# A hybrid decoder layer: the sample states are multiplied as they were loaded, in float32 and by column groups, and the new value's share is added at the end

## The chip, the cores and the metric

The kernel runs on one core of a Trainium2 chip. The metric is the device time of one execution in microseconds (us), lower is better. A measurement is the median of several runs. One execution was taken with the hardware profiler; its span is the time from the first to the last instruction of the program, and its own time is a little longer.

## The reference

One layer of a decoder is computed for a prompt of 512 tokens and for eight samples of one token each, which share all weights: 520 columns of activations in all, d_model 1024. The layer has one input projection, a dilated sliding-window attention (A), a gated linear attention (B), a merge by gates, an output projection, and a feed-forward block with squared relu; then a final RMSNorm. The change lies mainly in B for the samples:

```python
def gla_recurrent(q, k, v, g, s0):
    def step(state, inp):
        qt, kt, vt, gt = inp
        state = jnp.exp(gt)[..., None] * state + kt[..., None] * vt[:, :, None, :]
        return state, jnp.einsum('bhd,bhdv->bhv', qt, state)
...
def rmsnorm(x, g):
    xf = x.astype(jnp.float32)
    y = xf * lax.rsqrt(jnp.mean(xf * xf, axis=-1, keepdims=True) + EPS)
    return (y * g.astype(jnp.float32)).astype(x.dtype)
```

There are eight samples and four heads; a state is 128 x 256 float32 (128 KB), so that 32 states, 4 MB, are read, updated and written back. With a = exp(g), the output is o = q (diag(a) S + k v), which is also (q * a) S + (q . k) v.

## The kernel before

**Layout.** Activations lie with features on the 128 partitions, as tiles of 8 x 520 columns; the 520 columns are two halves of 260 (256 prompt tokens and four samples each). Weights come as panels of 128 output columns: `load_panel` fetches 512 KB on SP's queue, `split_panel` (L78) makes a high part on ACT (L90) and the rest on DVE (L91), and `panel_mms` (L106) multiplies in three passes of fp32r matmuls (L124), 48 matmuls of 260 columns a panel. TensorE goes through 140 panels in this way, and the rest of the work is woven between them.

**Fillers.** Work beside the panels stands in Python generators. `fill` (L130) takes steps of the generators in turn, `rate` steps after each panel; a step ends at `yield`. In the stage of B, `heads()` steps through `gla` (the prompt's chunked form, four heads after one another) and `samples()` through `gla_s` (L662) and `gla_s_out`, at four steps a panel; a generator that isn't ready yields True and costs no step.

**Order.** All instructions are handed to a planner, which sets the order on each engine by a simulated timeline, with the order of the program as priority. On the chip, each engine takes its instructions in the planned order and waits at each for its semaphores. A DMA stands in the queue of the engine that issues it: loads on SP's, the outputs of states and the cache copies on POOL's.

**gla_s, by head.** The preparing step makes the decay `a` (128 x 8) from the gate, copies k and q of the samples to `kq`, transposes v to rows (L679) and writes them to a DRAM tile `dV`. The next step makes `qs`, where q of a sample stands as a high and a low column of a 16-column weight, the others zero (L685 to L687). Then, for each pair of samples, the states are loaded to `st` (`sst`, two buffers, L692), the value rows are broadcast to `vb` (L693), ACT multiplies vb by k (L696), DVE makes the new state in `st` (L697), ACT and POOL split it into hi and lo in the buffer `gx` (L701, L702), four matmuls (L706) add to `po`, and POOL issues the output of `st` (L708). At the head's end `po` (16 x 256) is copied (L711), transposed (L714), and the high and low halves are added to `oS` (L715).

**The start.** `start` (L192) loads x in eight tiles and the first panels, and splits x times the norm's weight into `uh` (ACT, L211) and `ul` (DVE, L212). `stats` (L218) squares x on ACT (L223, L224), adds pairs on DVE (L225), and sums over partitions with a matmul by ones (L227), in four sets. `late_consts` (L232) loads seven small constants on POOL's queue. `rsqrt` (L174) makes v = scale * ss + eps on DVE (L179), Ln and Exp on ACT, and a Newton step on DVE.

**The end.** For each half, after the last panels (L968), the squares are summed (L979, L980), `rsqrt` gives `rs`, and `dd` is multiplied by it, six tiles on DVE and two on POOL (L985), with an output for each two tiles (L987).

Of the kernel before, what the change touches and what calls it, by code (L numbers as in the profile page):

```python
# [9 lines left out]
F32 = mybir.dt.float32  # L10
# [34 lines left out]
class Build:  # L45
# [116 lines left out]
    def pace(self, n=1):  # L162

        for _ in range(n):
            if self.copies:
                o, i = self.copies.pop(0)
                c = self.nc.gpsimd.dma_start(o, i)
                if self.last is not None:
                    self.tc.add_manual_dep(
                        c.ins, self.last.ins.name,  # L170
                        mybir.DependencyInfo(mybir.DependencyClass.Sync, mybir.DependencyReason.DATA),
                        reason="pace")

    def rsqrt(self, pool, out, ss, n, scale, np_=P):  # L174
# [3 lines left out]
        a = pool.tile([P, n], F32, tag=f"ra{n}", name="ra")  # L178
        nc.vector.tensor_scalar(v[:np_], ss, scale, EPS, op0=ALU.mult, op1=ALU.add)  # L179
        nc.scalar.activation(a[:np_], ss, AF.Ln, scale=scale, bias=self.eps[:np_])  # L180
# [11 lines left out]
    def start(self):  # L192
# [17 lines left out]
        for k in range(KT):  # L210
            nc.scalar.activation(self.uh[:, k], xr[:, k], AF.Copy, scale=self.g("n1", k))  # L211
# [6 lines left out]
    def stats(self, ap, xr):  # L218
        nc = self.nc
        pr = self.ps.tile([P, 2, 512], F32, tag="rps", name="rps")  # L220
        for k in range(0, KT, 2):
            a, b = (ap.tile([P, NT], F32, tag="sq", name="sq", bufs=5) for _ in range(2))
            nc.scalar.activation(a, xr[:, k], AF.Square)  # L223
            nc.scalar.activation(b, xr[:, k + 1], AF.Square)  # L224
            nc.vector.tensor_tensor(a, a, b, op=ALU.add)  # L225
            for j in range(2):
                nc.tensor.matmul(pr[:, j, :HC], self.ones, a[:, j * HC:(j + 1) * HC], start=(k == 0), stop=(k == KT - 2))  # L227
# [4 lines left out]
    def late_consts(self):  # L232
        nc, cp, I = self.nc, self.cp, self.I
        for n in ("ident", "maskN", "maskC", "qmask", "hsel", "dmask", "lmask"):
            a = I[n]
            t = cp.tile(list(a.shape), U8 if n == "lmask" else F32, tag=n, name=n)
            nc.gpsimd.dma_start(t, a)
# [424 lines left out]
    def gla_s(self, gp):  # L662
        nc, I, O = self.nc, self.I, self.O
        oS = gp.tile([P, 4, 2, NB], F32, tag="oS", name="oS", bufs=1)
        for h in range(4):
# [10 lines left out]
            vs = gp.tile([P, 2, 256], F32, tag="svb", name="vs", bufs=2)[:NB, 0]  # L676
# [4 lines left out]
            nc.sync.dma_start(dV, vs)  # L681
            yield

            qs = self.gx[:, :16 * NB]
            nc.scalar.activation(qs, self.ones, AF.Copy, scale=0.0)  # L685
            nc.scalar.activation(qs[:, 0::17], kq[:, 1], AF.Copy)
            nc.vector.tensor_tensor(qs[:, 8::17], kq[:, 1], qs[:, 0::17].bitcast(F32), op=ALU.subtract)  # L687
            po = self.bank("gso")
            for bp in range(4):
                st = gp.tile([P, 2, 256], F32, tag="sst", name="sst", bufs=2)  # L690
                vb = gp.tile([P, 2, 256], F32, tag="svb", name="svb", bufs=2)
                nc.sync.dma_start(st, I["state"][2 * bp:2 * bp + 2, h].rearrange("b d v -> d b v"))  # L692
                nc.sync.dma_start(vb, dV[2 * bp:2 * bp + 2].unsqueeze(0).to_broadcast([P, 2, 256]))  # L693
                for i in range(2):
                    b = 2 * bp + i
                    nc.scalar.activation(vb[:, i], vb[:, i], AF.Copy, scale=kq[:, 0, b:b + 1])  # L696
                    nc.vector.scalar_tensor_tensor(st[:, i], st[:, i], a[:, b:b + 1], vb[:, i],  # L697
                                                   op0=ALU.mult, op1=ALU.add)
                x = P + 1024 * (bp % 2)
                hi, lo = (self.gx[:, y:y + 512].rearrange("p (i v) -> p i v", i=2) for y in (x, x + 512))  # L700
                nc.scalar.activation(hi, st, AF.Copy)  # L701
                nc.gpsimd.tensor_tensor(lo, st, hi.bitcast(F32), op=ALU.subtract)  # L702
                for i in range(2):
                    b = 2 * bp + i
                    for n, w in enumerate((hi, lo)):
                        nc.tensor.matmul(po[:16, :256], qs[:, 16 * b:16 * b + 16], w[:, i],  # L706
                                         start=(b == 0 and n == 0), stop=(b == NB - 1 and n == 1))
                nc.gpsimd.dma_start(O["sgla"][2 * bp:2 * bp + 2, h].rearrange("b d v -> d b v"), st)  # L708
                yield
            o16 = gp.tile([P, 256], F32, tag="state", name="o16", bufs=2)[:16]  # L710
            nc.scalar.activation(o16, po[:16, :256], AF.Copy)  # L711
            pt = self.bank("gsp")
            for x in range(2):
                nc.tensor.transpose(pt[:, 16 * x:16 * x + 16], o16[:, x * P:(x + 1) * P], self.c["ident"][:16, :16])  # L714
            nc.vector.tensor_reduce(oS[:, h], pt[:, :32].rearrange("p (x n b) -> p x b n", x=2, n=2), axis=AX, op=ALU.add)  # L715
            yield
        sq = gp.tile([P, 4, 2, NB], F32, tag="sqS", name="sqS", bufs=1)
        nc.vector.tensor_tensor(sq, oS, oS, op=ALU.mult)
# [34 lines left out]
    def run(self):  # L753
# [74 lines left out]
        def gla_parts():  # L828
# [4 lines left out]
            self.gx = self.big("gx", F32R).rearrange("p a b -> p (a b)")  # L833
# [46 lines left out]
        with pool("late") as p:  # L880
# [75 lines left out]
            for j in range(2):  # L956
# [26 lines left out]
                for k in range(KT):  # L983
                    eng = nc.gpsimd if k >= 6 else nc.vector
                    eng.tensor_tensor(dd[:, k, cc], dd[:, k, cc], rs, op=ALU.mult)  # L985
                    if k % 2:
                        nc.sync.dma_start(O["yT"][:, k - 1:k + 1, cc], dd[:, k - 1:k + 1, cc])  # L987
# [148 lines left out]
```

## Time and profile before

| what | value |
|---|---|
| median of 3 runs | 969.25 us (967.69 to 971.42) |
| the profiled execution's own time | 968.6 us |
| its span | 966.8 us |
| busy: PE, DVE, ACT, POOL | 928.8, 556.5, 389.8, 102.3 us |
| mean granted clock of TensorE | 0.985 |
| DMA | 155.28 MB, mean 161 GB/s |

The page of the profile shows the span in 40 slices, with a digit for the busy tenths of each engine and for the granted clock in tenths of full speed, and the chain of work that ended last by engine and line. Matmuls are pipelined, so that a matmul's own duration (about 0.28 us) is longer than the time from its start to the next one's. Rows of a group end with the idle time of the engine just before its instructions, and with what ended it; a row of the timeline has start, duration, engine and line, and in brackets the idle time before it. PE is TensorE's matmul, PEld its weight load, SPq, ACTq and POOLq are the queues of the issuing engines.

### The profile page before, as it was taken

To read this page: it belongs to the slowest core of one execution; us is meant where nothing else is said; L and a number is where in the kernel's file an instruction comes from. 1 tells how busy PE (TensorE), PEld (TensorE's weight loads), DVE (VectorE), ACT (ScalarE), POOL (GpSimd) and SP (SyncE) were. 2 spreads that over 40 slices of the span, in tenths; PEclk is the share of its full clock that TensorE was granted. 3 is DMA by queue.
4 is the path that set the end of the run, shared out by engine and by line. 5 is a ranking of instruction groups with operands and counts; after the bars stand their busy time and mean duration, and the time that the engine had idled before them with its cause. 6 is when DMAs were issued, how large, how long until landed. Compare 5 with 4: busy or idle time off the path is not lost.

```text
span 966.8 us, 19936 instructions
## 1 busy us (share of the span) xinstructions
PE 928.8 (96%) x8288; PEld 909.0 (94%) x8288; DVE 556.5 (58%) x1075; ACT 389.8 (40%) x760; POOL 102.3 (11%) x148
## 2 busy tenths in 40 slices
PE   6999999999998999899899999999999999999994
PEld 6999999999898988789899999999999999999993
DVE  6657747645866946748665556443443344555654
ACT  6233243352644545556633444422432243224532
POOL 1000000001323322311000000010000000000000
PEclk9999999998999999899999999999999999999997
DMA  7455735322445344211468776778775222323311
GB/s 237 149 200 201 227 114 189 111 66 70 154 133 180 116 149 147 78 53 64 160 240 305 261 262 218 278 265 306 262 261 197 88 87 90 108 88 109 110 46 44
DMA packets 38988, 155.28 MB, mean 161 GB/s; under 512 B 5561, under 2 KB 11969, under 8 KB 36946
## 3 DMA queue, kind: packets, MB, share of 16 engines
q1 hardware_dynamic: 33778, 95.26, 28.7%
q0 software_dynamic: 4976, 58.74, 17.7%
q8 instruction: 65, 1.06, 0.5%
q14 instruction: 25, 0.20, 0.1%
q10 hardware_dynamic: 144, 0.01, 0.0%
HBM read 140.66 MB, written 54.17 MB: 202 GB/s over the span
## 4 chain that ended last, share of the span: by engine, by line
PE 83%; DMA 5%; DVE 4%; issue 3%; POOL 2%; ACT 2%; SPq 0%; DVEq 0%; POOLq 0%; ACTq 0%
PE mps L124 69%; PE mps L968 5%; PE pvp L358 1%; DMA svb<-dV 1%; DMA sst<-in_state 1%; POOL gx L702 1%; DMA raw<-in_w_in 1%; PE ptp L347 1%; DMA QTt<-ro 1%; DMA out_sgla<-sst 1%; PE spO L151 1%; PE vps L298 1%; DVE wlo L91 1%; POOL out_sgla L708 1%; PE sps L332 0%
## 5 line engine op out<-in xcount | busy, mean ns | idle before, releaser
L90 ACT ACTIVATE whi<-raw 128x512 fp32r<-128x512 f32 x264 | 165.7, 629 | 361.3 <-PE mps L124 309.7
L91 DVE TENSOR_TENSOR wlo<-raw,whi 128x512 fp32r<-128x512 f32 x264 | 184.8, 701 | 148.9 <-ACT whi L90 147.3
L124 PE MATMUL mps<-uh,whi 128*128 128x260 f32 x928 | 194.4, 289 | 7.4 <-ACT whi L90 5.5
L124 PE MATMUL mps<-ul,whi 128*128 128x260 f32 x928 | 195.8, 290 | 0.0
L124 PE MATMUL mps<-uh,wlo 128*128 128x260 f32 x928 | 193.2, 288 | 0.0
L124 PEld LDWEIGHTS mps<-uh,whi 128*128 128x128 f32 x928 | 145.8, 191 | 8.4 <-ACT whi L90 5.5
L124 PEld LDWEIGHTS mps<-ul,whi 128*128 128x128 f32 x928 | 146.5, 191 | 2.6 <-issue 1.4
L124 PEld LDWEIGHTS mps<-uh,wlo 128*128 128x128 f32 x928 | 146.2, 191 | 1.8 <-issue 1.1
L124 PE MATMUL mps<-hh,whi 128*128 128x260 f32 x512 | 103.2, 283 | 0.0
L124 PE MATMUL mps<-hh,wlo 128*128 128x260 f32 x512 | 103.2, 283 | 0.0
L124 PE MATMUL mps<-hl,whi 128*128 128x260 f32 x512 | 103.0, 283 | 0.0
L124 PEld LDWEIGHTS mps<-hh,whi 128*128 128x128 f32 x512 | 79.0, 188 | 0.1
L124 PEld LDWEIGHTS mps<-hh,wlo 128*128 128x128 f32 x512 | 78.9, 188 | 0.0
L124 PEld LDWEIGHTS mps<-hl,whi 128*128 128x128 f32 x512 | 78.7, 188 | 0.0
L124 PE MATMUL mps<-fh,wlo 128*128 128x260 f32 x384 | 77.3, 283 | 0.0
L124 PE MATMUL mps<-fl,whi 128*128 128x260 f32 x384 | 77.2, 283 | 0.0
L124 PE MATMUL mps<-fh,whi 128*128 128x260 f32 x384 | 76.8, 282 | 0.0
L124 PEld LDWEIGHTS mps<-fh,wlo 128*128 128x128 f32 x384 | 59.2, 188 | 0.0
L124 PEld LDWEIGHTS mps<-fl,whi 128*128 128x128 f32 x384 | 59.0, 188 | 0.0
L124 PEld LDWEIGHTS mps<-fh,whi 128*128 128x128 f32 x384 | 59.0, 188 | 0.0
L968 PE MATMUL mps<-fh,lw 128*128 128x260 f32 x256 | 46.6, 283 | 0.0
L968 PEld LDWEIGHTS mps<-fh,lw 128*128 128x128 f32 x256 | 39.6, 188 | 0.1
(330 smaller groups left out, 1377.6 us busy)
## 6 DMA issues: line engine op xcount, KB each, us to landing
raw<-in_w_in SPq DMA_DIRECT2D x57, 512.0 KB, 3.6
raw<-in_w_up SPq DMA_DIRECT2D x32, 512.0 KB, 4.2
raw<-in_w_down SPq DMA_DIRECT2D x32, 512.0 KB, 4.6
sst<-in_state SPq DMA_DIRECT2D x16, 256.0 KB, 2.7
svb<-dV SPq DMA_DIRECT2D x16, 256.0 KB, 3.5
out_sgla<-sst POOLq DMA_DIRECT2D x16, 256.0 KB, 3.7
raw<-in_w_pb SPq DMA_DIRECT2D x8, 512.0 KB, 4.4
raw<-in_w_o SPq DMA_DIRECT2D x8, 512.0 KB, 5.7
```

The lines of the kernel that those rows point to most:

```text
L90: nc.scalar.activation(hi, raw[:, x:x + n], AF.Copy)
L91: nc.vector.tensor_tensor(lo, raw[:, x:x + n], hi.bitcast(F32), op=ALU.subtract)
L124: self.last = nc.tensor.matmul(out[j], w, x[:, k, j * HC:(j + 1) * HC], start=(k == 0 and n == 0), stop=(k == kt - 1 and n == 2))
L151: self.nc.tensor.matmul(*args, **kw)
L298: nc.tensor.transpose(pt[:, r * P:(r + 1) * P], vt[:, r * P:(r + 1) * P], self.c["ident"])
L347: nc.tensor.transpose(pt[:, hh, x], prs[hp][:, hh, x * P:(x + 1) * P], self.c["ident"])
L358: nc.tensor.matmul(po[:, hh * 64:hh * 64 + 64], prT[:, hh, x], v, start=(x == first), stop=(x == 1))
L702: nc.gpsimd.tensor_tensor(lo, st, hi.bitcast(F32), op=ALU.subtract)
L708: nc.gpsimd.dma_start(O["sgla"][2 * bp:2 * bp + 2, h].rearrange("b d v -> d b v"), st)
L968: nc.tensor.matmul(ps, w, x[:, kk, cc], start=(kk == 0 and n == 0), stop=(kk == KT - 1 and n == 2))
```

## The change

In `gla_s`, q times the decay stands in `qz`, a weight of 32 columns a sample, of which one is not zero. It multiplies the state as it was loaded, in float32, and four samples write to the four groups of 32 output partitions of `po`, the two halves of the samples to its two halves of 256 columns. The decayed and updated state is written over `vb`, which is what goes out. States and value rows of four samples are loaded at once (512 KB each), into halves of a large buffer `sx` that takes the place of `gx`, one step of the generator ahead of their use. At a head's end, `po` is copied whole and transposed in four blocks, of which every 32nd column is kept. After the last head, q . k is summed by a matmul with ones, and multiplied by v and added to `oS`.

The other edits: Ln is put ahead of v in `rsqrt`; the odd tiles' squares of x go to POOL, and four squares are added before the sum by ones, so that there are two sets of it; the seven constant loads wait for the last split of x; at the end, DVE multiplies two tiles of `dd` at a time, and POOL none.

```diff
     def rsqrt(self, pool, out, ss, n, scale, np_=P):
...
+        nc.scalar.activation(a[:np_], ss, AF.Ln, scale=scale, bias=self.eps[:np_])
         nc.vector.tensor_scalar(v[:np_], ss, scale, EPS, op0=ALU.mult, op1=ALU.add)
-        nc.scalar.activation(a[:np_], ss, AF.Ln, scale=scale, bias=self.eps[:np_])
         nc.scalar.activation(out, a[:np_], AF.Exp, scale=-0.5)
...
         for k in range(0, KT, 2):
-            a, b = (ap.tile([P, NT], F32, tag="sq", name="sq", bufs=5) for _ in range(2))
+            a, b = (ap.tile([P, NT], F32, tag="sq", name="sq", bufs=6) for _ in range(2))
             nc.scalar.activation(a, xr[:, k], AF.Square)
-            nc.scalar.activation(b, xr[:, k + 1], AF.Square)
+            nc.gpsimd.tensor_tensor(b, xr[:, k + 1], xr[:, k + 1], op=ALU.mult)
             nc.vector.tensor_tensor(a, a, b, op=ALU.add)
+            if k % 4 == 0:
+                first = a
+                continue
+            nc.vector.tensor_tensor(a, a, first, op=ALU.add)
             for j in range(2):
-                nc.tensor.matmul(pr[:, j, :HC], self.ones, a[:, j * HC:(j + 1) * HC], start=(k == 0), stop=(k == KT - 2))
+                nc.tensor.matmul(pr[:, j, :HC], self.ones, a[:, j * HC:(j + 1) * HC], start=(k == 2), stop=(k == KT - 2))
...
-            nc.gpsimd.dma_start(t, a)
+            self.after(nc.gpsimd.dma_start(t, a), self.split_x)
...
     def gla_s(self, gp):
...
+        qz = gp.tile([P, NB, 32], F32, tag="qz", name="qz", bufs=1)
+        nc.gpsimd.memset(qz, 0.0)
+        qk = gp.tile([P, 4, NB], F32, tag="qk", name="qk", bufs=1)
...
             nc.sync.dma_start(dV, vs)
+
+            nc.vector.tensor_tensor(qz[:, :, 0], kq[:, 1], a, op=ALU.mult)
+            nc.vector.tensor_tensor(qk[:, h], kq[:, 1], kq[:, 0], op=ALU.mult)
             yield
-
-            qs = self.gx[:, :16 * NB]
-            nc.scalar.activation(qs, self.ones, AF.Copy, scale=0.0)
-            nc.scalar.activation(qs[:, 0::17], kq[:, 1], AF.Copy)
-            nc.vector.tensor_tensor(qs[:, 8::17], kq[:, 1], qs[:, 0::17].bitcast(F32), op=ALU.subtract)
             po = self.bank("gso")
-            for bp in range(4):
...
+            for bh in range(2):
+                bs = slice(4 * bh, 4 * bh + 4)
+                st, vb = (self.sx[:, x:x + 1024].rearrange("p (b v) -> p b v", b=4)
+                          for x in (1024 * bh, 2048 + 1024 * bh))
+                nc.sync.dma_start(st, I["state"][bs, h].rearrange("b d v -> d b v"))
+                nc.sync.dma_start(vb, dV[bs].unsqueeze(0).to_broadcast([P, 4, 256]))
+                yield
+
+                for i in range(4):
+                    nc.tensor.matmul(po[32 * i:32 * i + 32, 256 * bh:256 * bh + 256], qz[:, 4 * bh + i], st[:, i],
+                                     start=True, stop=True)
+                for i in range(4):
+                    b = 4 * bh + i
                     nc.scalar.activation(vb[:, i], vb[:, i], AF.Copy, scale=kq[:, 0, b:b + 1])
-                    nc.vector.scalar_tensor_tensor(st[:, i], st[:, i], a[:, b:b + 1], vb[:, i],
+                    nc.vector.scalar_tensor_tensor(vb[:, i], st[:, i], a[:, b:b + 1], vb[:, i],
                                                    op0=ALU.mult, op1=ALU.add)
-                x = P + 1024 * (bp % 2)
-                hi, lo = (self.gx[:, y:y + 512].rearrange("p (i v) -> p i v", i=2) for y in (x, x + 512))
-                nc.scalar.activation(hi, st, AF.Copy)
-                nc.gpsimd.tensor_tensor(lo, st, hi.bitcast(F32), op=ALU.subtract)
-                for i in range(2):
-                    b = 2 * bp + i
-                    for n, w in enumerate((hi, lo)):
-                        nc.tensor.matmul(po[:16, :256], qs[:, 16 * b:16 * b + 16], w[:, i],
-                                         start=(b == 0 and n == 0), stop=(b == NB - 1 and n == 1))
-                nc.gpsimd.dma_start(O["sgla"][2 * bp:2 * bp + 2, h].rearrange("b d v -> d b v"), st)
+                nc.gpsimd.dma_start(O["sgla"][bs, h].rearrange("b d v -> d b v"), vb)
                 yield
-            o16 = gp.tile([P, 256], F32, tag="state", name="o16", bufs=2)[:16]
-            nc.scalar.activation(o16, po[:16, :256], AF.Copy)
+            ov = gp.tile([P, 512], F32, tag="ov", name="ov", bufs=1)
+            nc.scalar.activation(ov, po, AF.Copy)
             pt = self.bank("gsp")
             for x in range(2):
-                nc.tensor.transpose(pt[:, 16 * x:16 * x + 16], o16[:, x * P:(x + 1) * P], self.c["ident"][:16, :16])
-            nc.vector.tensor_reduce(oS[:, h], pt[:, :32].rearrange("p (x n b) -> p x b n", x=2, n=2), axis=AX, op=ALU.add)
+                for bh in range(2):
+                    y = 256 * bh + P * x
+                    nc.tensor.transpose(pt[:, P * (2 * x + bh):P * (2 * x + bh + 1)], ov[:, y:y + P], self.c["ident"])
+            nc.vector.tensor_copy(oS[:, h], pt.rearrange("p (x u) -> p x u", x=2)[:, :, 0::32])
             yield
         sq = gp.tile([P, 4, 2, NB], F32, tag="sqS", name="sqS", bufs=1)
+        pk = self.bank("gqk")
+        nc.tensor.matmul(pk[:, :32], self.ones, qk.rearrange("p h b -> p (h b)"), start=True, stop=True)
+        nc.vector.tensor_tensor(sq, self.SVb.rearrange("p (h x) b -> p h x b", x=2),
+                                pk[:, :32].rearrange("p (h b) -> p h b", h=4).unsqueeze(2).to_broadcast([P, 4, 2, NB]),
+                                op=ALU.mult)
+        nc.vector.tensor_tensor(oS, oS, sq, op=ALU.add)
...
-            self.gx = self.big("gx", F32R).rearrange("p a b -> p (a b)")
+            self.sx = self.big("sx").rearrange("p a b -> p (a b)")
...
-                for k in range(KT):
-                    eng = nc.gpsimd if k >= 6 else nc.vector
-                    eng.tensor_tensor(dd[:, k, cc], dd[:, k, cc], rs, op=ALU.mult)
-                    if k % 2:
-                        nc.sync.dma_start(O["yT"][:, k - 1:k + 1, cc], dd[:, k - 1:k + 1, cc])
+                for k in range(0, KT, 2):
+                    ks = slice(k, k + 2)
+                    nc.vector.tensor_tensor(dd[:, ks, cc], dd[:, ks, cc], rs.unsqueeze(1).to_broadcast([P, 2, HC]),
+                                            op=ALU.mult)
+                    nc.sync.dma_start(O["yT"][:, ks, cc], dd[:, ks, cc])
```

`self.after(a, b)` makes a wait for b; it is the code that `pace` had, as a function. `self.split_x` is the last of the eight instructions of L211. The value rows `vs` get a buffer of their own.

More of the change, by code (lines that the diff above doesn't have):

```diff
@@ L168, in pace, with after @@
                 if self.last is not None:
[L169 to L172, printed above, removed]
+                    self.after(c, self.last)
+    def after(self, a, b):
+        self.tc.add_manual_dep(a.ins, b.ins.name,
+                               mybir.DependencyInfo(mybir.DependencyClass.Sync, mybir.DependencyReason.DATA),
+                               reason="pace")
     def rsqrt(self, pool, out, ss, n, scale, np_=P):
@@ L210, in start @@
         for k in range(KT):
-            nc.scalar.activation(self.uh[:, k], xr[:, k], AF.Copy, scale=self.g("n1", k))
+            self.split_x = nc.scalar.activation(self.uh[:, k], xr[:, k], AF.Copy, scale=self.g("n1", k))
             nc.vector.scalar_tensor_tensor(self.ul[:, k], xr[:, k], self.g("n1", k), self.uh[:, k].bitcast(F32),
@@ L675, in gla_s @@
             dV = self.dp.tile([NB, 256], F32, tag="dV", name="dV", bufs=2)
-            vs = gp.tile([P, 2, 256], F32, tag="svb", name="vs", bufs=2)[:NB, 0]
+            vs = gp.tile([P, 256], F32, tag="vs", name="vs", bufs=1)[:NB]
             pt = self.bank("vsp")
@@ L681, in gla_s @@
             nc.sync.dma_start(dV, vs)
+            nc.vector.tensor_tensor(qz[:, :, 0], kq[:, 1], a, op=ALU.mult)
+            nc.vector.tensor_tensor(qk[:, h], kq[:, 1], kq[:, 0], op=ALU.mult)
             yield
-            qs = self.gx[:, :16 * NB]
-            nc.scalar.activation(qs, self.ones, AF.Copy, scale=0.0)
-            nc.scalar.activation(qs[:, 0::17], kq[:, 1], AF.Copy)
-            nc.vector.tensor_tensor(qs[:, 8::17], kq[:, 1], qs[:, 0::17].bitcast(F32), op=ALU.subtract)
             po = self.bank("gso")
-            for bp in range(4):
[L690 to L693, printed above, removed]
-                for i in range(2):
-                    b = 2 * bp + i
+            for bh in range(2):
[10 more added lines that the diff above has]
+                    b = 4 * bh + i
@@ L701, in gla_s @@
[L701 to L704, printed above, removed]
-                    for n, w in enumerate((hi, lo)):
-                        nc.tensor.matmul(po[:16, :256], qs[:, 16 * b:16 * b + 16], w[:, i],
-                                         start=(b == 0 and n == 0), stop=(b == NB - 1 and n == 1))
-                nc.gpsimd.dma_start(O["sgla"][2 * bp:2 * bp + 2, h].rearrange("b d v -> d b v"), st)
+                nc.gpsimd.dma_start(O["sgla"][bs, h].rearrange("b d v -> d b v"), vb)
```

## The prediction

> **What bounds the kernel now.** I read the page first, then the chain of waits, then what PE waited for, and then the stages at which the change works.
>
> ```profile
> span 966.8 us, 19936 instructions
> ...
> PE   6999999999998999899899999999999999999994
> ...
> DVE  6657747645866946748665556443443344555654
> ...
> PEclk9999999998999999899999999999999999999997
> ...
> PE 83%; DMA 5%; DVE 4%; issue 3%; POOL 2%; ACT 2%; SPq 0%; DVEq 0%; POOLq 0%; ACTq 0%
> ```
>
> PE carries 83% of the chain. It falls short in three places: the first slice, slices 11 to 20 (245 to 485 us, where both gated-linear-attention generators are woven between the weight panels), and the last. A saving counts only if it takes PE work or PE waits out of these; elsewhere PE is full. The chain gives PE's pace:
>
> ```profile
> 484.78 102.37 PE mps L124 x852
> ```
>
> That is 102.37 / 852 = 0.120 us a panel matmul. In the middle stage PE waits, by the view of its waits, for this among others:
>
> ```profile
> PE gso L706 <- ACT gx L701: 3.1, 5, 1.2
> PE gop L656 <- DVE os L651: 2.7, 2, 2.0
> PE gso L706 <- POOL gx L702: 2.7, 3, 1.2
> PE lev L545 <- DVE D L607: 2.1, 3, 1.5
> ```
>
> Eight of the sixteen pairs of samples held PE, 3.1 + 2.7 = 5.8 us, for the split of the new state into hi and lo. A further wait, at klp, is POOL's too: the timeline has gx and kl one behind the other on POOL, drawn out to 2.83 and 3.46 us, and PE standing 1.95 for the second.
>
> ```profile
> 389.62 2.83 POOL L702 TENSOR_TENSOR gx<-sst,gx 128x512 fp32r<-128x512 f32 x1
> 392.41 3.46 POOL L572 TENSOR_TENSOR kl<-kl,QKb 128x512 f32<-128x512 f32 x1
> 395.93 1.12 PE L575 MATMUL klp<-ident,kl 128*128 128x128 f32 x4 [1.95 <-POOL kl L572]
> ```
>
> Right there the granted clock falls to half. A window put on it (busy time of PE, PEld, DVE, ACT, POOL, then the clock) shows 0.51:
>
> ```profile
> 395.10:402.00 6.90, 6.07 (x90) 5.55 (x91) 4.33 (x11) 1.64 (x4) 2.45 (x2) 0.51 0.23 78
> ```
>
> 6.9 us at half speed cost 3.4 more.
>
> **The sample states, PE work.** Per head, 16 matmuls of a 16-column weight (fp32r) become 8 fp32 matmuls, each two records, in groups of four at output partitions 0, 32, 64 and 96. Two 16-row transposes become four full ones. No row shows 256 columns in column groups; the nearest do 32 columns in groups, and 256 columns alone:
>
> ```profile
> 257.25 0.36 PE L706 MATMUL gso<-gx 128*16 128x256 f32 x1
> 257.54 0.46 PE L545 MATMUL lev<-QKb 128*32 128x32 f32 x32
> 257.81 0.48 PE L545 MATMUL lev<-D,QKb 128*32 128x16 f32 x32
> ...
> 350.17 0.51 PE L706 MATMUL gso<-gx 128*16 128x256 f32 x3
> 350.52 0.28 PE L124 MATMUL mps<-ul,whi 128*128 128x260 f32 x1
> ...
> 354.23 0.59 PE L636 MATMUL gpu<-Vb,klT 128*128 128x256 f32 x2
> 354.66 0.60 PE L298 MATMUL vps<-ident,vt 128*128 128x128 f32 x4
> 355.02 0.37 PE L124 MATMUL mps<-ul,whi 128*128 128x260 f32 x1
> ```
>
> From start to start, fp32 with 256 columns takes (354.66 - 354.23) / 2 = 0.215 us a record, 0.027 for 32 columns. Thirty-two records one after another would be 0.86 us; they took 257.81 - 257.54 = 0.27, so four ran at once. A group of four at 256 columns is then two passes, 0.43 us; one after another it would be 1.72. The old matmul took (350.52 - 350.17) / 3 = 0.117. Going into the column groups has a price: gso at 257.25 to lev at 257.54 is 0.29, some 0.17 over 0.117. The Trainium skill, TensorEngine Tiling (Array Packing), under Key Properties, says that changing the tiling mode drains the engine, which speaks against eight short visits; this row agrees. Without a drain the new work would be 2.7 us less. I take eight groups and 16 switches: 8 x 0.43 + 16 x 0.17 = 6.2 us. Sixteen transposes at (355.02 - 354.66) / 4, about 0.1, are 1.6, and the ones-matmul for q.k, two short records, 0.1: together 7.9. Before: 64 x 0.117 = 7.5, and eight small transposes at the same 0.1, 0.8: 8.3. **PE work -0.4**, with ends -3.1 (no price for going in and out) and +9.9 (groups one after another). I keep close to the lev rows, since they are the same form with fewer columns.
>
> **The sample states, waits.** The new products need only qz (DVE, in the preparing step) and the state as loaded, one yield earlier than now. So the 16 splits on ACT and the 16 on POOL leave, the latter worth
>
> ```profile
> L702 POOL TENSOR_TENSOR gx<-sst,gx 128x512 fp32r<-128x512 f32 x16 | 24.0, 1501 | 2.6 <-ACT gx L701 1.9 <-issue 0.5
> ```
>
> and the decay update leaves PE's path: it feeds the output alone. DVE keeps its 32 updates; per head it loses a subtraction and a sum of 32 columns and gets two products of 8 columns and a copy of 16, with two products at the end: about as much as before, under the idle tenths of its row on the page (four to nine busy). ACT copies 128x512 out of PSUM where it copied 16x256, and loses two copies for qs beside the splits. POOL gets one memset and issues eight outputs in place of 16, each still behind a DVE update. None of these holds PE; where DVE were full, its few tenths a head would be some 1 us in all. Gone: 5.8 us of gso waits. What is late next is the load, and behind a gso that waits on PE stand all panel matmuls. From the waits of DVE and of SP, and from the page's issues:
>
> ```profile
> DVE sst L697 <- DMA sst<-in_state: 6.8, 5, 3.3
> SPq L692 <- DMA out_sgla<-sst: 34.1, 9, 6.7
> raw<-in_w_in SPq DMA_DIRECT2D x57, 512.0 KB, 3.6
> sst<-in_state SPq DMA_DIRECT2D x16, 256.0 KB, 2.7
> ```
>
> Five loads were late, 1.4 us on average, because a buffer came back only after its own output had left: SP stood 34.1 us behind that, with weight loads behind it. Now the state is not overwritten; its half of sx is free once the previous head's update has read it, and only the vb load waits for an output, a head older. A load of twice the size takes about 3.6 us by the weight panel's row, and has that of lead if SP issues it a step ahead. I give back two of eight groups at 5.8 / 8 = 0.73: +1.5. Ends: 0, and all eight at 3.6 (a rival). **-4.3.**
>
> POOL's kl no longer stands behind gx. PE arrives sooner too, by the gso waits ahead of it (1.2 us the longest), so I credit half of the klp wait, -1.0, and half of the 3.4 us of slow clock, **-1.7**; ends nothing and -5.3. The waits for os and D I leave, though DVE is freed. Two rows of the timelines of POOL and DVE show from what:
>
> ```profile
> 268.35 1.31 POOL L702 TENSOR_TENSOR gx<-sst,gx 128x512 fp32r<-128x512 f32 x1
> ...
> 268.47 1.74 DVE L602 TENSOR_TENSOR D<-cum 128x512 f32<-128x512 f32 x1
> ```
>
> POOL ends at 269.66, DVE at 270.21: of its 1.74 us the product ran 0.55 alone, and stood for the rest. The Trainium skill, SBUF — State Buffer, under SBUF: two separate sides, calls the port pair of these two engines an exclusive lock; the row agrees. With that the term's end would be -4.8, the waits for os and D.
>
> **The start.** Eight of 16 records of the ones-matmul go, since four squares are added up first:
>
> ```profile
> 17.72 1.69 PE mps L124 x14
> 19.41 0.88 PE rps L227 x4
> ```
>
> Two of four sets of 0.88 are -1.8. The seven constant loads leave the first 13 us, in which the DMA engines are full, and wait on POOL's queue for ACT's last split of x. Behind them on POOL comes nothing before the first kT output, unless the order sets a square there; their first readers are proj_v's transposes, two rope pairs later. PE's second start hangs on the second half of panel 0:
>
> ```profile
> 0.00:13.00 13.00, 5.63 (x19) 4.72 (x20) 5.70 (x9) 8.31 (x14) 4.34 (x13) 1.00 0.87 288
> ...
> maskN<-in_maskN POOLq DMA_DIRECT2D x1, 128.0 KB, 5.2
> ...
> ident<-in_ident POOLq DMA_DIRECT2D x1, 64.0 KB, 4.1
> ```
>
> ```profile
> 7.74 0.63 ACT L90 ACTIVATE whi<-raw 128x512 fp32r<-128x512 f32 x1 [2.34 <-DMA raw<-in_w_in]
> ...
> 9.04 0.80 PE L124 MATMUL mps<-uh,whi 128*128 128x260 f32 x2 [1.91 <-ACT uh L211]
> ...
> 15.91 0.76 DVE L212 SCALAR_TENSOR_TENSOR ul<-xr,gcols,uh 128x520 fp32r<-128x520 f32 x1 [0.26 <-ACT uh L211]
> ```
>
> With these 192 KB no longer ahead of it at 288 GB/s (the last column of the window) it comes up to 0.7 us sooner; I take 0.5. Against that, four squares move to POOL (1.3 us and up, by the row above) and hold DVE's ul. The last ul is ready at 15.91 + 0.76 = 16.7 and read late in the batch that starts at 17.72, at about 18.5; ACT, rid of four squares, hands uh over sooner, and PE comes 2.3 sooner. I take 1.0 us of new wait. The last sum is due on PE at 19.41 - 2.3 = 17.1; up to there POOL's squares are hidden. **-1.3**, ends -2.3 and +3.
>
> **The end.** rsqrt's Ln no longer stands behind v, and four products of 520 columns replace six on DVE and two on POOL:
>
> ```profile
> 954.05 0.43 DVE L179 TENSOR_SCALAR rv<-r 128x260 f32<-128x260 f32 x1 [1.25 <-PE r L980]
> ...
> 956.87 3.20 DVE L985 TENSOR_TENSOR dd<-dd,rs 128x260 f32<-128x260 f32 x6
> ```
>
> ```profile
> L939 DVE TENSOR_TENSOR dd<-dd,rv 128x520 f32<-128x520 f32 x8 | 5.5, 693 | 0.0
> ```
>
> -0.43 and a hand-over for v, some -0.5; 4 x 0.69 = 2.8 in place of 3.20, -0.4. **-0.9**, ends -0.5 and -1.3.
>
> **Sum.** -0.4 - 4.3 - 1.0 - 1.7 - 1.3 - 0.9 = -9.6. The profiled execution took 968.6 (its span and 1.8 around it): 959.0. It lies 0.65 under the median of 969.25, within the spread of the three; I leave the sum at 959.0.
>
> **The rivals.** (A) The heads' own chains take it back. PE reaches klp, lev and gop sooner, but those wait for scans, exponentials and DVE: all of the 5.8, the klp wait and the clock are lost, and -0.4 - 1.3 - 0.9 = -2.6 stays: 966.0. For it: those waits stand beside gso's now. Against: POOL's and ACT's work on the same chains goes. (B) POOL's squares hold DVE at the start, as gx did at 268.35: four of 1.31, all ahead of ul, make 5.2 us of stall, less the 2.3 saved: +2.9 in place of -1.3, 963.2. It decides once ul is over 1.8 us late. This is what the Trainium skill's lock (SBUF — State Buffer, SBUF: two separate sides) would do here. (C) Slower: PE waits for st itself, in front of every group, because SP issues each load only when its step comes up: 959.0 - 1.5 + 8 x 2.7 = 979.1. The price is the present landing of a load. It makes the kernel slower from (974.1 - 957.5) / 8 = 2.1 us a group. For it: five loads were late. Against: the buffer rule is looser, and a load precedes its use by a step. (D) The four groups run one after another, so the change doesn't do what it says: 8 x (1.72 - 0.43) = 10.3 over the forecast, 969.3. Against: the lev rows.
>
> **How the numbers follow.** Forecast 0.62, A 0.16, B 0.08, C 0.08, D 0.04, and 0.02 for less than the range. A measurement of this kernel can tell about 0.5%, 4.8 us, from no change: faster is under 964.4, slower over 974.1. Faster: 0.62 + 0.06 of A + 0.05 of B + 0.02 = 0.75. Same: 0.10 of A, 0.03 of B, 0.03 of D = 0.16. Slower: C and 0.01 of D = 0.09. The low end takes the terms' good ends in part (-3.1 - 5.8 - 5.3 - 2.3 - 1.3 = -17.8, 950.8, and os and D beyond): 950; the high end covers A and B: 968.
>
> **What would show it.** gso's records in fours, groups 0.43 us apart and the wait before them under 1 us; no POOL product between 245 and 400 but qe and kl; clock 1.0 around klp; rps in two sets and no PE wait for ul or rps before 20 us; the last dd 0.9 us sooner after r. A PE wait on in_state, or gop and lev waits grown by what gso lost, would make it wrong.

## The result, and the profile after

The changed kernel takes 947.01 us (median of 4 runs, 943.87 to 949.30); the kernel before took 970.34 us beside it (4 runs, 967.69 to 971.50). The ratio is 0.977, with a 95% interval of 0.973 to 0.980: 23 us faster, where 10 were forecast, and below the range. The profiled execution of after took 943.87, so that 24.7 us are to be found between the two profiles (968.6 before).

The page of after, with the rows that answer to those of before:

```profile
span 942.1 us, 19815 instructions
...
PE   6999999999999999999999999999999999999995
...
DVE  6756746844775958676755556433443344555664
...
PEclk9999999998999999999999999999999999999998
...
PE 96%; DVE 2%; issue 1%; ACT 1%; DMA 0%; SPq 0%; DVEq 0%; ACTq 0%
```

PE's share of the chain is 96% where it was 83%. The eights in slices 11 to 20 are gone from PE's row. To see how much came from where, cut both spans at three instants that every version has: the first zp matmul (the gates, where the stage of B begins), the first sum of squares after the output projection, and the last panel matmul. From PE's timelines (start, duration, engine, line), before:

```profile
242.92 1.02 PE L554 MATMUL zp<-G,wg 128*128 128x512 f32 x2
...
586.99 1.04 PE L928 MATMUL r<-acc,ones 128*128 128x260 f32 x4
...
951.59 0.28 PE L968 MATMUL mps<-fh,lw 128*128 128x260 f32 x1
```

and after:

```profile
244.07 1.02 PE L561 MATMUL zp<-G,wg 128*128 128x512 f32 x2
...
566.30 1.04 PE L941 MATMUL r<-acc,ones 128*128 128x260 f32 x4
...
930.90 0.28 PE L981 MATMUL mps<-fh,lw 128*128 128x260 f32 x1
```

| stretch | before | after | difference | forecast |
|---|---|---|---|---|
| span's start to zp | 242.92 | 244.07 | +1.2 | -1.3 |
| zp to the sum of squares (the middle stage) | 344.07 | 322.23 | -21.8 | -7.4 |
| to the last panel matmul | 364.60 | 364.60 | 0.0 | 0 |
| to the span's end (966.8, 942.1) | 15.2 | 11.2 | -4.0 | -0.9 |

The forecast of -7.4 is -0.4 - 4.3 - 1.0 - 1.7. So the gain lies in the middle stage, and some lies at the end. The +1.2 of the first row is within what two executions differ by there, as the section on the experiments shows. A window over exactly the middle stage says what kind of time went (columns: the window, its length, then busy time and instructions of PE, PEld, DVE, ACT, POOL, the granted clock, DMA share, GB/s). Before:

```profile
242.92:586.98 344.06, 328.13 (x3324) 314.14 (x3323) 226.35 (x465) 170.95 (x350) 69.35 (x81) 0.99 0.48 165
```

and after:

```profile
244.07:566.30 322.23, 320.31 (x3333) 307.06 (x3332) 217.38 (x470) 160.60 (x328) 36.72 (x57) 1.00 0.51 174
```

PE idle is the length less PE's busy time: 344.06 - 328.13 = 15.9 before, 322.23 - 320.31 = 1.9 after. That is 14.0 of the 21.8. The other 7.8 is busy time. Before had 6.9 us at half speed (in the prediction) and 3.4 more:

```profile
415.60:419.00 3.40, 3.40 (x45) 3.34 (x34) 3.40 (x11) 1.27 (x2) 0.00 (x0) 0.50 0.16 27
```

PE was busy for 6.07 and 3.40 us of these two stretches. If the same work takes half as long at full speed, they cost 4.7 us of busy time, by estimate; after has no such stretch in this stage. About 3.1 us of the 7.8 are then left for less work. What PE still waits for in after, by the view of its waits over the whole span (total, times, longest):

```profile
PE mps L124 <- ACT whi L90: 5.3, 1, 5.3
PE mps L124 <- DVE ul L215: 1.9, 2, 1.3
...
PE lev L617 <- DVE D L614: 0.8, 1, 0.8
PE klp L582 <- POOL kl L579: 0.6, 1, 0.6
PE gso L706 <- PE lev L552: 0.5, 1, 0.5
```

The first is the program's start, and the same as before but for 0.2 us. Within the middle stage, the waits put down to gso fell from 5.8 to 0.5 us and klp's from 1.9 to 0.6. The waits of the heads for os, D, jk and vps, which the change does not touch, fell from 8.1 to 0.8 us (before: 2.7 for os, 2.1 and 1.2 for D, 1.5 for jk, 0.6 for vps).

### The profile page after: what moved, and what is told of

Its sections match the earlier page's. It is cut to its first block, busy times and chain, and to the rows that moved or that the text cites. A ratio compares the mean times of both kernels' runs of the same rounds, so it can differ in the third digit from the quotient of the medians.

```text
span 942.1 us, 19815 instructions
## 1 busy us (share of the span) xinstructions
PE 921.9 (98%) x8290; PEld 902.7 (96%) x8290; DVE 550.0 (58%) x1079; ACT 376.7 (40%) x732; POOL 72.4 (8%) x125
## 4 chain that ended last, share of the span: by engine, by line
PE 96%; DVE 2%; issue 1%; ACT 1%; DMA 0%; SPq 0%; DVEq 0%; ACTq 0%
PE mps L124 80%; PE mps L981 5%; PE pvp L365 1%; PE lev L552 1%; PE ptp L354 1%; PE gpo L639 1%; PE gpu L643 1%; PE vps L305 1%; PE gso L706 1%; PE gpo L641 1%; PE spO L151 1%; PE sps L339 1%; DMA raw<-in_w_in 0%; PE mps L516 0%; PE sps L334 0%
## 5 line engine op out<-in xcount | busy, mean ns | idle before, releaser
L91 DVE TENSOR_TENSOR wlo<-raw,whi 128x512 fp32r<-128x512 f32 x264 | 182.4, 692 | 148.3 <-ACT whi L90 145.9
```

The lines of the kernel that those rows point to most:

```text
L91: nc.vector.tensor_tensor(lo, raw[:, x:x + n], hi.bitcast(F32), op=ALU.subtract)
```

## The experiments

The question was why the middle stage gave three times what was forecast. My theory: POOL's 16 splits (24.0 us) had held DVE, which the heads' chains wait for, so their removal freed the heads. Rivals: ACT's load fell, or the loads no longer stand behind outputs. Further runs take the start and the end apart.

Beside the first four runs the kernel before had a median of 969.96 us, beside the next four 970.89, and beside the last three 971.27. Runs of one kernel differ by 3 us and more. In the eight profiles of kernels that share after's start (after, e2 to e7 and e9), zp starts anywhere from 243.92 to 250.41 us; stages are therefore compared by the window over them.

**e2: POOL's products put back.** Sixteen subtractions on POOL, whose results nobody reads, in the changed kernel:

```diff
+                for y in range(0, 4, 2):
+                    jl = gp.tile([P, 2, 256], F32R, tag="jl", name="jl", bufs=2)
+                    nc.gpsimd.tensor_tensor(jl, st[:, y:y + 2], vb[:, y:y + 2], op=ALU.subtract)
```

> The changed kernel with 16 products of 128x512 put back on POOL in gla_s, each with two SBUF inputs, as many as the splits were, written to a tile that nobody reads. PE never waits for them. Theory 'port': they hold DVE and delay POOL's kl, which the planned order doesn't know; the PE waits of the heads (gop, lev, klp, gpu, 7 to 9 us before the change, 1.9 us after) come back, with stretches of half clock, 954 to 962 us. Rival 'ACT' (the splits on ACT were the cause) and rival 'SP' (loads that stood behind outputs): no difference, 945 to 949 us.

958.48 us (957.30 to 965.70), ratio 0.989 (0.985 to 0.993): half of the gain is gone. Its window over the middle stage:

```profile
246.68:581.66 334.98, 324.04 (x3333) 309.93 (x3332) 232.33 (x470) 161.06 (x328) 62.78 (x73) 0.99 0.49 168
```

PE idles 10.9 us in place of 1.9, its busy time is 3.7 more (the clock fell to half for 6.8 us), and the stage is 12.8 longer. DVE has the same 470 instructions as after and is busy 15.0 us longer with them. The timelines of POOL, DVE and PE show the hold at work:

```profile
259.23 1.91 DVE L711 SCALAR_TENSOR_TENSOR sx<-sx,as__2854 128x256 f32<-128x256 f32 x2
259.31 1.55 POOL L715 TENSOR_TENSOR jl<-sx 128x512 fp32r<-128x512 f32 x1 [0.36 <-DVE kqs L684]
...
261.22 1.40 POOL L715 TENSOR_TENSOR jl<-sx 128x512 fp32r<-128x512 f32 x1 [0.36 <-DVE sx L711]
261.40 1.50 DVE L614 TENSOR_TENSOR D<-D,QKb 128x256 f32<-128x256 f32 x1
...
271.81 0.46 PE L552 MATMUL lev<-D 128*32 128x32 f32 x32 [2.06 <-DVE D L614]
```

The product at 261.40 takes 0.41 us when POOL is quiet (267.53 in the same timeline). Here it stands until POOL's, begun 0.18 us earlier, ends. The heads' chain of D goes through such products, and ten us later PE waits at lev. In the whole stage PE waits 5.8 us for D, where after has 0.8, and klp's wait is 1.4 in place of 0.6:

```profile
PE lev L552 <- DVE D L614: 5.8, 3, 3.0
```

Instructions that are added also change the planned order, but the order alone is not the price: of PE's 3331 matmuls in the stage some 2620 stand in after's sequence in e2 and 2650 in e3 (below), which adds as many instructions on ACT, and e3's stage is 0.5 us longer.

**e11: the split taken off POOL in the kernel before.** The counter-test: DVE gets 16 instructions more, POOL 16 fewer, and nothing else changes.

```diff
-                nc.gpsimd.tensor_tensor(lo, st, hi.bitcast(F32), op=ALU.subtract)
+                nc.vector.tensor_tensor(lo, st, hi.bitcast(F32), op=ALU.subtract)
```

> The kernel before, with only the lo half of the state split moved from POOL to DVE; PE's work is the same. Theory 'POOL's products held DVE': the waits of the heads for os, D, jk and the stretches of half clock go although DVE gets 16 x 0.69 = 11 us of work more; the middle stage falls from 344.1 to 330 to 336 us, the time to 957 to 963. Rival 'DVE is just the fuller engine': DVE's added 11 us lengthen the heads' chains, the stage is 344 or more and the time 969 to 978. gso's waits for the split stay in both, now on DVE.

964.30 us (962.00 to 968.47), ratio 0.994 (0.992 to 0.996): faster than before, though DVE has more to do. The size was missed: the stage is 1.4 us over the range, the time 1.3.

```profile
243.30:580.74 337.44, 325.42 (x3324) 312.38 (x3323) 227.09 (x481) 170.31 (x350) 42.79 (x65) 0.99 0.49 168
```

Sixteen more instructions of 0.68 us each should add 10.9 us to DVE's busy time; it went from 226.35 to 227.09. DVE had thus been standing 10 us. PE idles 12.0 us in place of 15.9, but one part of the expectation failed: the heads' waits did not go.

```profile
PE lev L545 <- DVE D L607: 4.2, 5, 2.0
PE gop L656 <- DVE os L651: 2.0, 1, 2.0
```

With those for jk and vps they come to 8.8 us in the stage, where before had 8.1. What fell is gso's wait (5.8 to 2.9), klp's (1.9 to 0.2; POOL's kl has no split ahead of it any more), and the time at half clock (10.2 to 3.4 us). DVE is as long occupied as in before, now with work in place of standing. So taking the products off POOL did not free the heads here, where DVE got them instead. Over the runs, the heads' waits go with DVE's busy time in the stage: 8 to 9 us of them at 226 to 232 us (before, e11, e2), 0.8 at 217 and 215 (after, e10).

**e10: no product on POOL in the middle stage at all.** The version e1 (below) with the heads' products for qe and kl on DVE too:

```diff
-        nc.gpsimd.tensor_tensor(qe, qe, q, op=ALU.mult)
+        nc.vector.tensor_tensor(qe, qe, q, op=ALU.mult)
...
-        nc.gpsimd.tensor_tensor(kl, kl, k, op=ALU.mult)
+        nc.vector.tensor_tensor(kl, kl, k, op=ALU.mult)
```

> The version with the odd squares back on ACT, and the heads' two products for qe and kl on DVE in place of POOL, so that POOL makes no product in the middle stage. Theory 'POOL's products hold DVE': DVE's own two products a head (16 x 0.69 = 11 us) are about what it stands for POOL's 16 today, the klp wait of 0.6 us goes: 941 to 943.5 against 943.5. Rival 'DVE's queue is what the heads wait for': the waits for D, kl and os grow, the stage by 3 us or more, 946 to 950.

941.35 us (937.64 to 947.86), ratio 0.971 (0.968 to 0.974). The expectation counted 16 products; four heads have eight.

```profile
242.43:563.58 321.15, 320.35 (x3332) 307.14 (x3331) 214.73 (x478) 160.50 (x328) 22.88 (x49) 1.00 0.51 175
```

DVE does eight products more and is busy 2.7 us less than in after, and PE idles 0.8 us in the whole stage. Against e1 (943.52) the times alone don't decide: the intervals of the ratios overlap. It is the fastest median of the study.

**e9: POOL busy without reading.** Three memsets in place of each product of e2, to see whether reading is what holds DVE, or POOL's queue what holds klp.

```diff
+                for y in range(0, 4, 2):
+                    jm = gp.tile([P, 512], F32, tag="jm", name="jm", bufs=2)
+                    for z in range(3):
+                        nc.gpsimd.memset(jm, 0.0)
```

> The changed kernel with 48 memsets of 128x512 put on POOL in gla_s (three where the last experiment had a product), to a tile that nobody reads. POOL is about as long busy as with the 16 products, but reads nothing. Theory 'port' (POOL's reads of SBUF hold DVE's products with two inputs): no difference to the changed kernel, 944 to 950 us. Rival 'POOL's queue' (kl and qe come late behind other work on POOL): PE waits at klp and half clock, 952 to 962 us, as with the products.

952.41 us (950.24 to 956.51), ratio 0.982 (0.979 to 0.985). A miss: the memsets cost more than the range allowed, and the time lies at the low end of the rival's. The rival's mechanism did not come, though: klp's wait is 0.6 us, as in after. The stage is 6.1 us longer than after's, with 6.8 us at half clock and one wait of 3.7 us. The timelines show the stand behind it, one that I had not thought possible:

```profile
264.89 6.61 POOL L716 MEMSET jm<- 128x512 f32 x14
265.04 0.68 DVE L91 TENSOR_TENSOR wlo<-raw,whi 128x512 fp32r<-128x512 f32 x1
...
265.64 5.88 DVE L536 COPY SVb<-vt 128x8 f32<-128x8 f32 x1
265.72 5.81 DVE L91 TENSOR_TENSOR wlo<-raw,whi 128x512 fp32r<-128x512 f32 x1
...
266.52 5.02 DVE L609 TENSOR_TENSOR D<-cum 128x512 f32<-128x512 f32 x1
...
272.05 0.65 PE L622 MATMUL lev<-D 128*32 128x32 f32 x16 [3.74 <-DVE sd L602]
```

Fourteen memsets in a row did not touch the product of two inputs at 265.04 (0.68 us, its usual time), but a copy of eight columns (0.16 us in e2, at 268.47) stood 5.88 us until they ended, and everything in DVE's queue behind it stood too. The Trainium skill, SBUF — State Buffer, under SBUF: two separate sides, makes this distinction: a vector instruction with two SBUF inputs contends only with a POOL instruction that reads SBUF, one in a two-port mode with any. The trace agrees on the first, with 0.68 us. The 5.88 us fit the second if the copy ran in such a mode, which no trace shows.

**e3: ACT's load put back.** Sixteen copies of 128x512 on ACT that nobody reads:

```diff
+                for y in range(0, 4, 2):
+                    jh = gp.tile([P, 2, 256], F32R, tag="jh", name="jh", bufs=2)
+                    nc.scalar.activation(jh, vb[:, y:y + 2], AF.Copy)
```

> The changed kernel with 16 copies of 128x512 put back on ACT in gla_s, as many as the high parts were, written to a tile that nobody reads. Theory 'port' and rival 'SP': no difference, 945 to 949 us. Rival 'ACT': the exponentials and splits on ACT come late, the heads' PE waits come back, 952 to 960 us.

947.22 us (946.20 to 949.18), ratio 0.976 (0.973 to 0.979): as after. Its middle stage:

```profile
247.43:570.17 322.74, 320.32 (x3333) 307.24 (x3331) 217.78 (x470) 168.72 (x344) 35.59 (x57) 1.00 0.50 174
```

ACT is busy 8.1 us more, the stage 0.5 longer. This rival falls.

**e6: one buffer for states and value rows.** Each load of value rows must wait until the output of the four samples before has read the buffer, and each load of states until their update has:

```diff
-                          for x in (1024 * bh, 2048 + 1024 * bh))
+                          for x in (0, 2048))
```

> The changed kernel with one buffer for states and value rows in place of two, so that each load of value rows waits on SP for the output of the four samples before, and each load of states for their update, as the loads before the change waited for outputs (34.1 us of SP). Theory 'port': such waits cost little, 946 to 951 us. Rival 'SP': the weight loads behind them come late and gso waits for the states: 8 waits of 1.5 to 3 us, 958 to 970 us.

954.23 us (951.76 to 956.65), ratio 0.983 (0.980 to 0.986), between the two theories. From its timeline and its window:

```profile
272.43 0.64 PE L706 MATMUL gso<-sx,qz 128*32 128x256 f32 x8 [1.75 <-DMA sx<-in_state]
```

```profile
247.37:578.04 330.67, 323.43 (x3333) 310.41 (x3331) 218.50 (x470) 160.33 (x327) 34.46 (x57) 0.99 0.50 171
```

PE waited twice for a load (3.6 us in all), the clock fell to half for 6.8 us, and the stage grew by 8.4. This is stricter than before was, where two buffers stood behind one output each. It shows that the order of the loads has a worth of its own, not how much of it the change brought.

**e7: one column group.** All four samples' products go to output partitions 0 to 31. Each product overwrites the one before, and only those rows are copied out, so the recurrent outputs of most sample tokens are left out.

```diff
-                    nc.tensor.matmul(po[32 * i:32 * i + 32, 256 * bh:256 * bh + 256], qz[:, 4 * bh + i], st[:, i],
+                    nc.tensor.matmul(po[:32, 256 * bh:256 * bh + 256], qz[:, 4 * bh + i], st[:, i],
```

> All 64 state products write output partitions 0 to 31, one column group instead of four; only those 32 rows are copied out, so the recurrent outputs of the sample tokens beyond each head's first 32 rows are left out (they stay zero). Theory 'four at once': a group of 8 records, 0.48 us in the changed kernel, becomes 8 x 0.215 = 1.72 us, so 8 groups cost 8 x 1.24 = 9.9 us more: the middle stage 332 us in place of 322.2, the time 955 to 959. Rival 'the groups run one after another anyway, the 0.48 us is only the short records': groups stay at 0.5 us and the time within 945 to 949. A third, 'PE time is hidden by waits': groups grow, but the stage by less than 4 us.

959.11 us (954.37 to 959.85), ratio 0.987 (0.984 to 0.989): 0.1 past the upper end of what the theory has. One group of eight records in PE's timeline of e7, with what follows it:

```profile
266.05 0.39 PE L708 MATMUL gso<-sx,qz 128*32 128x256 f32 x1
...
266.27 1.67 PE L708 MATMUL gso<-sx,qz 128*32 128x256 f32 x7
267.87 0.68 PE L617 MATMUL lev<-D 128*64 128x64 f32 x8
```

and the same place in after:

```profile
259.71 0.39 PE L706 MATMUL gso<-sx,qz 128*32 128x256 f32 x1
...
259.74 0.62 PE L706 MATMUL gso<-sx,qz 128*32 128x256 f32 x6
260.29 0.68 PE L617 MATMUL lev<-D 128*64 128x64 f32 x8
```

From the first record to what follows it takes 267.87 - 266.05 = 1.82 us in one column group and 260.29 - 259.71 = 0.58 in four, so four ran at once. Eight times the difference is 9.9; the stage grew by 9.7 (331.9 by its window). The profiled executions differ by 16.0 us; the other 6.3 lie ahead of zp (250.4 in its profile), in work that the edit doesn't touch.

**e8: the sample states alone.** The kernel before with the new `gla_s` and the buffer `sx` and none of the other edits.

> The kernel before with the new gla_s alone: start, rsqrt, constants and end as before. Theory: the parts add up. The stretch from the first zp to the sum of squares behind w_o takes 322 us as in the changed kernel (344 before), the start and the last 15 us are those of before: 948 us, 946 to 950. Rival 'the plan of the middle stage hangs on the other edits': that stretch differs by over 3 us from 322, and the time by as much from 948.

951.20 us (948.55 to 953.41), ratio 0.981 (0.978 to 0.983), 1.2 over the range.

```profile
245.55:567.42 321.87, 320.13 (x3334) 307.23 (x3333) 217.58 (x470) 160.02 (x328) 37.32 (x57) 1.00 0.50 174
```

The middle stage is that of after, the end still long (14.6 us): the gain of the stage doesn't hang on the other edits.

**e1: the odd squares back on ACT.** The changed kernel, with its two sets of sums:

```diff
-            nc.gpsimd.tensor_tensor(b, xr[:, k + 1], xr[:, k + 1], op=ALU.mult)
+            nc.scalar.activation(b, xr[:, k + 1], AF.Square)
```

> The changed kernel with the odd squares of x back on ACT (two sets of sums kept). Theory 'POOL holds DVE at the start': the PE waits for ul and uh before 20 us (1.9 + 0.4 us) go, the clock is full from about 13 us where it was from 17.5, and the kernel is 3 to 5 us faster than the changed one, 942 to 944 us. Rival 'the start is set by the loads of x and of panel 0': no difference, 946 to 948 us.

943.52 us (942.22 to 945.22), ratio 0.972 (0.969 to 0.975), as my theory had it; but its interval just overlaps that of after (0.973 to 0.980), and the profiled executions are alike (944.12 and 943.87). The start of after, from the timelines of POOL, DVE and PE:

```profile
6.68 4.51 POOL L227 TENSOR_TENSOR sq<-xr 128x520 f32<-128x520 f32 x3 [5.71 <-DMA xr<-in_xT]
...
7.39 1.42 DVE L215 SCALAR_TENSOR_TENSOR ul<-xr,gcols,uh 128x520 fp32r<-128x520 f32 x1
...
10.20 2.22 DVE L215 SCALAR_TENSOR_TENSOR ul<-xr,gcols,uh 128x520 fp32r<-128x520 f32 x2
...
11.80 0.80 PE L124 MATMUL mps<-ul,whi 128*128 128x260 f32 x2 [1.27 <-DVE ul L215]
...
13.11 1.51 POOL L227 TENSOR_TENSOR sq<-xr 128x520 f32<-128x520 f32 x1 [1.92 <-DVE sq L228]
```

and of e1:

```profile
7.60 0.76 DVE L215 SCALAR_TENSOR_TENSOR ul<-xr,gcols,uh 128x520 fp32r<-128x520 f32 x1 [0.41 <-ACT uh L214]
...
12.31 0.40 PE L124 MATMUL mps<-ul,whi 128*128 128x260 f32 x2
```

Where POOL squares, ul takes 1.42 in place of 0.76. PE waits, and its pairs of matmuls keep the slow pace (0.64 us a pair as late as 16.49), while e1's run at 0.40 from 12.31 on. The expectation called this the clock; the granted clock in the profiles is 1.00 from 12 to 18 us in both, so that it is shown by the pace alone. The first transpose of the values (vps) starts at 45.94 before, 47.73 after and 44.52 in e1. This holds beyond single profiles: 45.88 to 46.05 in the three with the old start (before, e8, e11), 46.90 to 48.06 in the eight with POOL's squares, 44.46 and 44.52 in the two with two sets of sums and ACT's squares (e10, e1). By zp the lead of e1 is gone again in the profiled execution (244.48, where after has 244.07), so what it is worth for the whole time is not settled.

**e4 and e5: the end.** e4 is the changed kernel with the old last multiply, six products on DVE and two on POOL:

```diff
-                    nc.vector.tensor_tensor(dd[:, ks, cc], dd[:, ks, cc], rs.unsqueeze(1).to_broadcast([P, 2, HC]),
-                                            op=ALU.mult)
+                    eng = nc.gpsimd if k >= 6 else nc.vector
+                    eng.tensor_tensor(dd[:, k, cc], dd[:, k, cc], rs, op=ALU.mult)
```

> The changed kernel with the old last multiply: six tiles on DVE and two on POOL for each half. Theory 'drain': POOL's closing drain takes about 9.05 us from POOL's last instruction, and sets the end when POOL works to the last: about 3.5 us longer, 950 to 951 us, with the last output landed as early as 0.7 us later than in the changed kernel. Rival 'lock only': DVE's products take 3.2 us in place of 2.5: 0.7 us longer, 947 to 948 us.

e5 keeps the new multiply, and has POOL multiply eight columns of the last `rs` by themselves, read by nobody:

```diff
+                if j:
+                    jk = p.tile([P, 8], F32, tag="jk", name="jk")
+                    nc.gpsimd.tensor_tensor(jk, rs[:, :8], rs[:, :8], op=ALU.mult)
```

> The changed kernel with one more product of 8 columns on POOL, of the last half's rs, to a tile that nobody reads. Theory 'drain': from the last panel matmul to the end of the span it takes about 14 us in place of 11.2, with POOL's drain of 8 to 9 us ending last and the last output landed no later. Rival 'the end is set by outputs and DVE': 11.2 us as in the changed kernel.

e4 took 947.88 us (946.72 to 950.42), ratio 0.977 (0.974 to 0.981), only 0.9 over after's median, which the runs can't resolve; by its time alone e4 would fit the rival. e5 took 947.58 in one run. The profiles resolve it: from the last panel matmul to the end it is 11.2 us in after, 14.1 in e4 and 13.0 in e5, where about 14 were expected. The program's closing instructions show why (name, count, least/median/greatest duration in ns, first and last start). Before, after, e4 and e5:

```profile
L1115 POOLq DRAIN  x3: 46/98/9051, 957.0 to 966.5; - x3
L1115 SPq DRAIN  x3: 7/7/7, 963.0 to 966.3; - x3
```

```profile
L1128 POOLq DRAIN  x3: 51/97/9079, 711.7 to 941.8; - x3
L1128 SPq DRAIN  x3: 7/7/7, 941.2 to 941.5; - x3
```

```profile
L1128 POOLq DRAIN  x3: 51/93/8397, 935.7 to 944.6; - x3
```

```profile
L1131 POOLq DRAIN  x3: 51/93/7222, 937.8 to 945.5; - x3
```

POOL ends with a drain of 7.2 to 9.1 us, which starts with its last work. Before, that ran from 957.0 to 966.0, when SP had its outputs behind it at 963.0: POOL set the end, by 3 us. In after it starts at 711.7 and is long over. In e5 a product of eight columns (0.57 us) is enough to bring 1.8 us back.

## Why the prediction was wrong, point by point

The sign held; the size did not. The largest part of the difference is in one place that was set to 0, the rest in the clock, PE's work and the end.

- **"The waits for os and D I leave, though DVE is freed."** This is the step that failed, and the largest. PE's idle time in the middle stage fell by 14.0 us: 5.3 of it is gso's (5.8 to 0.5), 1.3 klp's, and 7.3 the heads' waits for os, D, jk and vps (8.1 to 0.8). I had read the row in which a product of DVE stood for POOL's split, and had named its worth (-4.8 by two of these waits), but took 0. What the runs showed in its place: POOL's 16 splits had kept DVE standing for some 10 us of the stage (e11), and with 16 such products put back, DVE is busy 15.0 us longer, the heads' waits return (5.8 us at D alone) and the stage is 12.8 us longer (e2). ACT's load is not the cause (e3). How the 21.8 us share out beyond the waits named here is open: e11 gains 6.6 us without freeing the heads, the looser loads may have a part (e6), and no run puts POOL's products where the other kernel has them.
- **The slow clock, -1.7.** Half of one stretch was credited; both stretches went, some 4.7 us of PE's busy time. In the middle stage the half clock goes with PE's waits: after, e1, e3, e7, e8 and e10, where PE hardly waits, have none, and before, e2, e6, e9 and e11 have 3.4 to 10.2 us. That the waits bring it on is likely by this, not shown. If they do, they are not the only cause: every version has a stretch of 3.4 or 6.8 us at half clock between 221 and 236 us, ahead of the stage, and after's, from 222.3 to 229.1, has PE busy throughout.
- **The klp wait, -1.0.** It went from 1.9 to 0.6, -1.3. Near enough.
- **gso's waits, -4.3.** They went by 5.3; no wait of PE in after is put down to a load of states, so the 1.5 given back was not needed. Rival C had its condition in e6 only, and there two groups waited, not eight.
- **PE's work, -0.4.** The mechanism is as forecast: four at once, e7. Summed over the trace from start to start, the eight visits took 5.5 us, where 6.2 with the price for going in and out were taken; the one shown under e7 took 0.58. The drain on a change of tiling mode that the Trainium skill states (TensorEngine Tiling (Array Packing), Key Properties) is then small here: less the 0.43 of two passes, 0.58 and the mean of 5.5 / 8 = 0.69 leave 0.15 to 0.26 us for a visit, not 0.34. From start to start, the products and transposes of the samples took 9.5 us before, where 8.3 were taken, and 7.6 after with the matmul for q . k: the term measured -1.9 in place of -0.4. The rest of the 3.1 us of busy time was not followed.
- **The start, -1.3.** Rival B came instead, with a smaller price: the first vps is 1.8 us later, not 1.3 earlier. I had set 1.0 us of wait against POOL's squares because the late ul looked hidden; but the three squares in a row (4.51 us) met the first ul too, which PE was waiting for. e1 takes them off POOL and gives 45.94 - 44.52 = 1.4 us: 1.4 of the 2.3 us that were set down for the term's savings are there at vps once POOL doesn't square.
- **The end, -0.9.** Ln ahead of v and the four wide products gave 1.1, close to the forecast (3.20 to 2.53 in the products): SP's closing drain starts 11.4 us behind the last panel matmul before, 10.9 in e4 and 10.3 in after. The missing 2.9 is POOL's closing drain. The prediction looked at when the products were done, not at what the program still does after its last output, and the page of before has no row for it.
- **Rivals A and D** did not come: the heads' chains gained, and the groups don't run one after another.

The sum was built from waits that the change touches by name. What PE gained most from was waits that it touches through an engine two steps away, and those had been sized too small in two places: as a gain in the middle stage, set to 0, and as a cost at the start, set to 1.0. Both lead back to the hold of DVE by POOL, as far as the runs show it.

## What to carry to other kernels

When an edit moves work onto or off POOL, count DVE's stand too: compare the durations of one DVE instruction with and without POOL beside it, and follow what waits for DVE at both ends of the move. Moving POOL's elementwise products of SBUF operands to DVE can pay although DVE is the fuller engine (e11, 7 us by the medians); but DVE stayed as occupied there, and what waits for DVE gained nothing. Look at the last microseconds for POOL's drain before giving it any work there, however small.

## What the runs showed of the hardware that I had not expected

- POOL memsets, which read nothing, held a DVE copy of eight columns for 5.88 us, until the last of 14 had ended, and left a DVE product of two inputs alone (e9).
- POOL's drain at the end of the program takes 7.2 to 9.1 us from its last work in the four profiles shown, whatever that was (a product of eight columns in e5, the issue of a DMA in after).
- With some 2 us more of waits in the first 12 us, PE's full pace came about 5 us later: pairs of matmuls take 0.40 us from 12.31 on in e1, and still 0.64 at 16.49 in after, while the granted clock reads 1.00 in both. That the waits are the cause was not tried by itself.
